# Two fused blocks on one core: GpSimd's elementwise work in 256-column pieces, and two waits of the schedule moved

## The chip, the cores and the metric

The kernel runs on one core of a Trainium2 chip, in one launch. The metric is device time in microseconds (us), the median of three executions. All durations below are from one profiled execution of the kernel before; times in it count from the start of its span.

## The reference

Two blocks follow each other on 256 tokens of width 1024. The first is a mixer (a gated causal convolution beside attention with a forget gate), cross attention to a memory, and a squared-ReLU MLP. The second is a state-space mixer with a short convolution, and then a product-key expert layer, which is the part that this study mostly speaks of:

```python
q = (t @ w_q).reshape(T, PEER_HEADS, 2, PEER_HALF)            # 8 heads
s = jnp.einsum('thsd,hskd->thsk', q, sub_keys)                # scores against 2 x 128 keys
v_half, i_half = lax.top_k(s, PEER_TOPK)                      # 16 of 128, per half
cand = v_half[:, :, 0, :, None] + v_half[:, :, 1, None, :]
best, pos = lax.top_k(cand, PEER_TOPK)                        # 16 of 256 pairs
experts = (i1 * PEER_KEYS + i2)                               # 16 experts per token and head
gates = jax.nn.softmax(best, axis=-1)
...
u = expert_u[eb]
act = jax.nn.gelu(jnp.einsum('td,tkd->tk', xb, u)) * gb
return jnp.einsum('tk,tkd->td', act, expert_v[eb])
```

Each of the 256 tokens reads 16 experts for each of 8 heads, and each expert is a row of u and a row of v, 1024 float32 numbers each.

## The kernel before

The 256 tokens are two tiles of 128 partitions. Nothing is issued where it is written: every operation is recorded in a `Plan`, and `Plan.schedule` places the recorded operations on the engines by a list scheduler with costs and priorities of its own, and `issue` then emits each engine's instructions in that order. Priorities come from the place of an operation in the program plus a shift for its block (`SHIFTS`, by block names such as `e03` or `scores1`). Some operations are recorded for `q.either` and may be placed on VectorE or GpSimd; `LATERS` holds for each block by how much the one engine must be ahead for the operation to go there. `q.wait` adds a predecessor that exists only for the scheduler: it moves instructions in the queues, and no engine waits for it at run time. All instructions are emitted from one line, so that the profile shows L519 nearly everywhere, and tiles tell them apart.

Matmuls in the first part take their weights in two parts: a rounded one, made by ScalarE, and the rest, made by a subtraction (`tensor_sub`) of 1024 columns on VectorE or GpSimd (`unit`). The scores of heads 1 to 7 use the same `unit` with `lead=0`; their subtractions go to VectorE alone, and they carry the scheduler's wait `q.place`.

The expert layer goes over tiles i and heads h in order; the blocks are e00 to e07 and e10 to e17 (tile, head). For each pair, `route` (blocks such as `route03`) finds the 16 experts of each token on VectorE from the scores `S[h]`; head 0 of tile 0 does it in haste, the first 8 experts ahead of the other 8. Then 16 gathers (`indirect_dma_start` on GpSimd's queue) each bring 128 rows of u and v, 2048 columns, into one of 10 row buffers. Per pair of rows VectorE makes the dot products (`dots`), ScalarE the gelu (`act`), VectorE multiplies by the gate, ScalarE scales the identity by the result (`dg`, two buffers), and TensorE multiplies `dg` with the v half and sums in two banks `acc`. The two matmuls that start `acc` add the residual `xt`. At the end of a tile the sum is normalised and stored. A row buffer is free for a later gather when the product has read it.

`HELD` weight units for the scores are loaded ahead and handed to `unit` through `early`.

Of the kernel before, what the change touches and what calls it, by code (L numbers as in the profile page):

```python
# [41 lines left out]
HELD = 10  # L42
# [37 lines left out]
    "attend21.te": 384, "mo.gp": 1722, "state3.ve": -1984, "ln.gp": 166, "dt.sy": 461, "dt.sc": 725,  # L80
# [127 lines left out]
class Plan:  # L208
# [163 lines left out]
    def schedule(self, window):  # L372
# [49 lines left out]
        while count < len(ops):  # L422
# [3 lines left out]
            for e in self.ENGINES:  # L426
                t0, pick = clock[e], None
                for i in cand[e]:
# [21 lines left out]
                    if not ok:  # L450
                        continue
# [1433 lines left out]
```

## Time and profile before

| | us |
|---|---|
| median of three runs | 1343.22 (1341.99 to 1345.15) |
| the profiled execution: its time | 1344.8 |
| its span in the profile | 1343.0 |
| first gather issued | 652.74 |
| last gather issued | 1314.08 |

The span is shorter than the time by what lies around it. The first 652.7 us hold the first block and the mixer of the second; the gathers of the expert layer take the rest.

### The profile page before, as it was taken

The numbers are of one execution on the slowest core, as the hardware profiler recorded it, in microseconds if no ns is written. First come the engines' busy times: TensorE is split into PE (matmuls) and PEld (weight loads), VectorE is DVE, ScalarE is ACT, GpSimd is POOL, SyncE is SP. The second block draws the span as 40 slices with busy tenths as digits, with TensorE's granted clock in tenths as the row PEclk, the third lists the DMA queues.
The fourth block names the chain that finished last, engine by engine and source line by source line (L and its number), as shares of the span: only waits on it lengthen the run. The fifth ranks groups of instructions, "written<-read, shape, count | busy, mean of one in ns | idle before, by whom it ended". The sixth has DMA issues, their size and how long they took to land.

```text
span 1343.0 us, 15842 instructions
## 1 busy us (share of the span) xinstructions
PE 1136.7 (85%) x5291; PEld 786.5 (59%) x5292; DVE 961.9 (72%) x2199; ACT 565.8 (42%) x1154; POOL 516.7 (38%) x405
## 2 busy tenths in 40 slices
PE   6998989999989989999497899887775977777776
PEld 5996778898969879988363555432332322222222
DVE  7988777555668887894789889997555455555555
ACT  6655565454545945653244444433222222112212
POOL 4731475220012574431333435554443533333330
PEclk9998999999989999999698999999997999999999
DMA  7432352555652334358588999999998999999996
GB/s 289 158 126 94 126 195 91 206 200 201 221 196 76 122 105 172 123 209 314 191 330 314 375 353 396 421 421 420 422 421 335 409 421 422 422 422 421 422 421 277
DMA packets 55701, 378.09 MB, mean 282 GB/s; under 512 B 6322, under 2 KB 6962, under 8 KB 11460
## 3 DMA queue, kind: packets, MB, share of 16 engines
q0 software_dynamic: 36864, 268.45, 48.8%
q1 hardware_dynamic: 18756, 108.63, 22.3%
q8 instruction: 42, 0.69, 0.2%
q14 instruction: 39, 0.32, 0.1%
HBM read 376.01 MB, written 1.05 MB: 281 GB/s over the span
## 4 chain that ended last, share of the span: by engine, by line
PE 37%; DMA 30%; DVE 17%; issue 7%; POOL 4%; ACT 4%; POOLq 0%; SPq 0%; DVEq 0%; ACTq 0%
DMA k<-in_uv,s_ei 28%; PE s L519 22%; PE mm L519 15%; DVE k L519 13%; POOL k L519 3%; ACT k L519 3%; DMA k<-in_wts 1%; DVE s_ix L519 1%; DVE s_v L519 1%; DMA x<-in_x 1%; DVE s_pos L519 1%; DVE act L519 1%; ACT L519 0%; DVE s_best L519 0%; POOL s_r L519 0%
## 5 line engine op out<-in xcount | busy, mean ns | idle before, releaser
L519 PE MATMUL s<-k,s_dg 128*128 128x512 f32 x1020 | 478.3, 616 | 148.6 <-ACT s_dg L519 148.4
L519 PEld LDWEIGHTS s<-k,s_dg 128*128 128x128 f32 x1020 | 189.8, 194 | 420.7 <-ACT s_dg L519 221.5
L519 DVE SCALAR_TENSOR_TENSOR k<-k,k 128x1024 bf16<-128x1024 f32 x256 | 312.9, 1222 | 168.5 <-DMA k<-in_uv,s_ei 167.9
L519 POOL DMA_INDIRECT k<-in_uv,s_ei x256 | 274.2, 1071 | 402.7 <-PE s L519 228.0
L519 PE MATMUL mm<-act,k 128*128 128x256 f32 (+4 forms) x2448 | 330.6, 288 | 2.7 <-ACT k L519 1.5
L519 PEld LDWEIGHTS mm<-act,k 128*128 128x128 f32 x2448 | 309.1, 189 | 17.1 <-issue 7.5
L519 ACT ACTIVATE k<-k 128x1024 fp32r<-128x1024 f32 (+9 forms) x293 | 230.3, 823 | 108.4 <-DVE k L519 63.8
L519 DVE TENSOR_TENSOR k<-k,k 128x1024 fp32r<-128x1024 f32 (+9 forms) x220 | 209.2, 982 | 45.7 <-ACT k L519 45.3
L519 POOL TENSOR_TENSOR k<-k,k 128x1024 fp32r<-128x1024 f32 (+4 forms) x84 | 180.5, 2166 | 152.8 <-ACT k L519 145.4
L519 PE MATMUL s<-k,k 128*128 128x512 f32 (+8 forms) x868 | 188.8, 362 | 10.7 <-DVE k L519 8.4
L519 ACT ACTIVATE s_act<-s_dots,rx 128x2 f32<-128x2 f32 x129 | 38.0, 294 | 337.1 <-DVE k L519 336.9
L519 PEld LDWEIGHTS s<-k,k 128*128 128x128 f32 (+2 forms) x868 | 145.2, 192 | 39.7 <-DVE k L519 9.5
L519 ACT ACTIVATE s_dg<-ident,s_act 128x128 f32<-128x128 f32 x255 | 91.6, 395 | 108.7 <-PE s L519 57.6
L519 PE MATMUL s<-k,act 128*128 128x512 f32 (+1 forms) x432 | 100.7, 382 | 1.6 <-ACT act L519 1.3
L519 PEld LDWEIGHTS s<-k,act 128*128 128x128 f32 x432 | 79.5, 193 | 13.0 <-ACT act L519 1.5
L519 ACT ACTIVATE k<-s 128x512 f32<-128x512 f32 (+10 forms) x99 | 46.3, 488 | 67.0 <-PE s L519 52.2
L519 DVE TENSOR_TENSOR k<-s,k 128x256 f32<-128x256 f32 (+8 forms) x100 | 45.1, 476 | 29.6 <-ACT k L519 21.2
L519 PE MATMUL s<-ident,k 128*128 128x128 f32 (+2 forms) x220 | 38.2, 302 | 26.9 <-DVE k L519 22.9
L519 ACT ACT_TABLE_LOAD x44 | 56.5, 1283 | 3.1 <-DVE s_mx L519 1.6
L519 ACT ACTIVATE k<-mm 128x256 f32<-128x256 f32 (+3 forms) x70 | 26.1, 373 | 67.8 <-PE mm L519 67.3
L519 POOL TENSOR_TENSOR s_r<-s_ms,nhalf 128x1 f32<-128x1 f32 x10 | 8.3, 835 | 102.2 <-DVE s_ms L519 98.5
L519 PEld LDWEIGHTS s<-ident,k 128*128 128x128 f32 (+2 forms) x220 | 27.5, 151 | 32.6 <-DVE k L519 25.0
(177 smaller groups left out, 778.9 us busy)
## 6 DMA issues: line engine op xcount, KB each, us to landing
k<-in_wts SPq DMA_DIRECT2D x89, 1024.0 KB, 4.8
k<-in_gains SPq DMA_DIRECT2D x9, 512.0 KB, 6.4
k<-in_uv,s_ei POOLq DMA_INDIRECT x256
k<-in_wts SPq DMA_DIRECT2D x12, 256.0 KB, 7.0
act<-in_wts SPq DMA_DIRECT2D x4, 512.0 KB, 9.4
x<-in_x SPq DMA_DIRECT2D x2, 512.0 KB, 6.7
k<-in_mem SPq DMA_DIRECT2D x2, 512.0 KB, 6.0
k<-in_sk SPq DMA_DIRECT2D x2, 512.0 KB, 6.0
```

Of the source, the lines that this page charges most:

```text
L519: getattr(getattr(self.nc, e), method)(*args, **kw)
```

## The change

There are four edits, and all numbers in `SHIFTS` (642 of 651) and most of `LATERS` (120 of 147) are other ones, so that all engines' queues are in a new order.

1. `cut`: an elementwise operation that is placed on GpSimd is emitted as pieces of at most 256 columns (`PIECE`). The scheduler's cost for GpSimd counts the pieces, and its rule for VectorE against GpSimd lets the other engine in between two pieces.
2. The wait of the matmuls that start `acc`: for the second tile it was the last recorded operation of the first tile, the store of its output; it is now `summed`, the last product of the first tile.
3. `q.place`, the wait of the scores of heads 1 to 7, was the last operation of the first two products of head 0, 1, 2 and 3; it is now the last operation of the scores of head 0.
4. `early.extend(held)` is done ahead of the loop.

```diff
+PIECE = 256
...
-            return 130 + 2.18 * n
+            return 130 * self.pieces(method, args, kw) + 2.18 * n
...
+    def pieces(self, method, args, kw):
+
+        if method not in ("tensor_sub", "tensor_mul", "tensor_add", "tensor_scalar") or "out" in kw:
+            return 1
+        shape = [c for _, c in args[0].ap]
+        if len(shape) == 2:
+            return max(1, -(-shape[1] // PIECE))
+        return max(1, -(-shape[1] * shape[2] // PIECE)) if len(shape) == 3 else 1
+
+    def cut(self, method, args, kw):
+
+        n = self.pieces(method, args, kw)
+        m = args[0].ap[1][1] if n > 1 else 1
+        step = -(-m // n)
+        for o in range(0, m, step):
+            yield args if n == 1 else tuple(
+                a[:, o:min(m, o + step)] if hasattr(a, "ap") and len(a.ap) > 1 and a.ap[1][1] == m else a
+                for a in args)
...
-                        r = max(r, lock["gpsimd" if e == "vector" else "vector"])
-                    s = max(r, t0)
+                        a, b, grain = lock["gpsimd" if e == "vector" else "vector"]
+                        if s < b:
+                            r = s = min(b, a + max(1, math.ceil((s - a) / grain)) * grain)
...
-                lock[e] = end
+                lock[e] = s, end, o.grain if e == "gpsimd" else 1e9
...
-            getattr(getattr(self.nc, e), method)(*args, **kw)
+            for a in self.cut(method, args, kw) if e == "gpsimd" else (args,):
+                getattr(getattr(self.nc, e), method)(*a, **kw)
...
     scores(0, whole=False)
+    early.extend(held)
+    st["next"] += HELD
+    q.place = q.last()
     q.block("experts")
...
-            q.wait = q.last()
+            q.wait = summed if i else q.last()
...
             if i == 0 and g == 0 and h < len(SCORES):
-                if h == 0:
-                    early.extend(held)
-                    st["next"] += HELD
-                q.place = q.last()
                 for x in SCORES[h]:
...
         if h == 7:
+            summed = q.last()
```

Of GpSimd's 66 elementwise operations on two tensors of 1024 columns, 44 stay and are emitted as four pieces each, and 22 go to VectorE; 12 multiplications of 256 columns go from VectorE to GpSimd.

The first place is the start of the second tile's head 0 (e10) on ScalarE. `s_act` is the gelu of two dot products, `s_dg` the scaled identity that a product waits for, and `k2` the square for the norm of the first tile. Before:

```order
L519 ACTIVATE s_act_2012<-s_dots_2007,rx1_1161 128x2
L519 ACTIVATE k2_2001,s_ss2_2000<-s_1220 128x512
L519 ACTIVATE k2_2002,s_ss2_2000<-s_1221 128x512
L519 ACTIVATE s_dg_2013<-ident_69,s_act_2012 128x128
L519 ACTIVATE s_dg_2014<-ident_69,s_act_2012 128x128
L519 ACTIVATE s_act_2020<-s_dots_2015,rx1_1161 128x2
L519 ACTIVATE s_act_2048<-s_dots_2043,rx1_1161 128x2
L519 ACTIVATE s_act_2056<-s_dots_2051,rx1_1161 128x2
L519 ACTIVATE s_act_2064<-s_dots_2059,rx1_1161 128x2
L519 ACTIVATE s_dg_2021<-ident_69,s_act_2020 128x128
```

Now:

```order
L548 ACTIVATE s_dg_2013<-ident_69,s_act_2012 128x128
L548 ACTIVATE s_dg_2014<-ident_69,s_act_2012 128x128
L548 ACTIVATE s_act_2020<-s_dots_2015,rx1_1161 128x2
L548 ACTIVATE s_dg_2021<-ident_69,s_act_2020 128x128
L548 ACTIVATE s_dg_2022<-ident_69,s_act_2020 128x128
L548 ACTIVATE s_act_2048<-s_dots_2043,rx1_1161 128x2
```

The scaled identity `s_dg_2021` stood behind three further gelus (of dot products of six later rows) and now follows its own.

The second place is TensorE between the scores of head 0 (`s_kp`) and the first product of the expert layer (the first row that names `s_dg`; `k_1223` is the first row buffer). `mm<-act` rows are matmuls for the scores of later heads. Before:

```order
L519 MATMUL s<-s_kp,k_1218 128x128 x2
L519 MATMUL s<-s_kp,k_1219 128x128
L519 MATMUL s<-x_63,ident 128x512 x2
L519 MATMUL s<-k_1223,s_dg 128x512 x2
L519 MATMUL s<-k_1224,s_dg 128x512 x2
L519 MATMUL s<-k_1259,s_dg 128x512 x2
L519 MATMUL s<-k_1260,s_dg 128x512 x2
L519 MATMUL s<-k_1287,s_dg 128x512
L519 MATMUL mm<-act,k_1236 128x256 x2
```

Now (the last rows ahead of the first product):

```order
L548 MATMUL s<-s_kp,k_1242 128x128
L548 MATMUL mm<-act,k_1475 128x256 x24
L548 MATMUL mm<-act,k_1250 128x256 x14
L548 MATMUL mm<-act,k_1479 128x256 x6
L548 MATMUL mm<-act,k_1250 128x256 x10
L548 MATMUL mm<-act,k_1479 128x256 x6
L548 MATMUL s<-s_kp,k_1252 128x128 x2
L548 MATMUL mm<-act,k_1479 128x256 x12
L548 MATMUL s<-s_kp,k_1253 128x128
L548 MATMUL s<-s_kp,k_1252 128x128 x2
L548 MATMUL s<-s_kp,k_1253 128x128
L548 MATMUL s<-k_1223,s_dg 128x512
```

Ahead of the first product stand 181 matmuls of the scores of heads 1, 2, 3 and 6, where none stood.

The third place is VectorE just ahead of the first list of experts, the cast to `s_ei_1199`, for which the first gather waits. Names with `s_v` and `s_ix` are another route's; rows that write a `k8` tile of 128x512 are the weights of the scores of heads 1 and 3, and `k1_1239` is a part of the scores of head 1. Before:

```order
L519 TENSOR_REDUCE s_pick_1196<-k2_1198 128x2x8
L519 CAST s_ixf_1935<-s_ix_1932 128x32
L519 TENSOR_TENSOR k1_1936<-s_v_1931 128x256
L519 SCALAR_TENSOR_TENSOR s_ef_1197<-s_pick_1196 128x8
L519 MAX_INDEX s_pos_1192<-s_best_1191,k1_1193 128x8
L519 MAX s_best_1937<-k1_1936 128x8
L519 CAST s_ei_1199<-s_ef_1197 128x8
```

Now:

```order
L548 TENSOR_REDUCE s_pick_1196<-k2_1198 128x2x8
L548 CAST s_abf_1195<-s_ab_1194 128x2x8
L548 TENSOR_SCALAR s_nb_1202<-s_best_1191,rx0_1160 128x1
L548 SCALAR_TENSOR_TENSOR s_ef_1197<-s_pick_1196 128x8
L548 TENSOR_TENSOR k2_1200<-s_abf_1195,iota16_76 128x128
L548 TENSOR_TENSOR k8_1348<-k2_1125,k8_1348 128x512
L548 TENSOR_TENSOR k1_1239<-mm_1237,k1_1238 128x256
L548 TENSOR_TENSOR k8_1348<-k2_1126,k8_1348 128x512
L548 CAST s_ei_1199<-s_ef_1197 128x8
```

Between the first maximum of this route and this cast stood 47 VectorE instructions, and now 52: eight more of the later heads' scores, eight fewer of the route of the second tile's head 0, and five more of this route's own second half.

Followed back through the queues and the waits, the first gather of e01, e02, e03, e04 and e05 has behind it 98, 168, 264, 349 and 447 VectorE instructions that come after those the first gather of all has behind it; now these are 91, 168, 200, 292 and 372.

## Rows read from the trace of the kernel before

**Rows 1.** The page: busy time by engine, and the gathers' DMA queue.
```profile
PE 1136.7 (85%) x5291; PEld 786.5 (59%) x5292; DVE 961.9 (72%) x2199; ACT 565.8 (42%) x1154; POOL 516.7 (38%) x405
...
q0 software_dynamic: 36864, 268.45, 48.8%
```
**Rows 2.** Windows (stretch, its length, busy us by engine, PE clock, DMA share, GB/s).
```profile
13.00:637.00 624.00, 592.60 (x3770) 532.65 (x3770) 472.32 (x842) 353.64 (x630) 233.98 (x130) 0.97 0.46 167
652.70:1343.00 690.30, 531.39 (x1448) 244.16 (x1448) 467.92 (x1273) 201.63 (x507) 276.30 (x258) 0.96 0.96 391
```
**Rows 3.** Windows from one head's first gather to the next's: e00 to e04, e10.
```profile
652.70:703.40 50.70, 36.13 (x156) 22.91 (x157) 38.72 (x125) 18.29 (x43) 20.34 (x18) 0.80 0.85 331
703.40:754.30 50.90, 41.12 (x145) 22.62 (x144) 46.32 (x157) 22.12 (x46) 18.01 (x17) 0.93 0.86 333
754.30:798.90 44.60, 39.38 (x160) 23.41 (x159) 37.63 (x120) 18.64 (x41) 18.75 (x16) 0.96 0.92 356
798.90:840.80 41.90, 39.69 (x158) 23.54 (x159) 40.53 (x135) 20.07 (x45) 19.72 (x16) 1.00 0.98 401
840.80:878.90 38.10, 33.00 (x96) 16.67 (x96) 38.10 (x148) 15.17 (x34) 19.94 (x16) 0.91 1.01 422
993.90:1045.20 51.30, 31.43 (x65) 12.84 (x66) 26.28 (x55) 12.77 (x35) 17.41 (x16) 0.87 0.88 357
```
**Rows 4.** Timeline of GpSimd: first gather, the one after the longest stop, last gather.
```profile
652.74 1.20 POOL L519 DMA_INDIRECT k<-in_uv,s_ei  x1 [17.02 <-DVE s_ab L519]
...
1038.37 0.93 POOL L519 DMA_INDIRECT k<-in_uv,s_ei  x1 [15.46 <-DVE k L519]
...
1314.08 0.94 POOL L519 DMA_INDIRECT k<-in_uv,s_ei  x1 [0.78 <-DVE k L519]
```
**Rows 5.** What TensorE's matmuls waited for, 13 to 637 us (us, times, longest).
```profile
PE s L519 <- DVE k L519: 31.5, 13, 12.6
```
**Rows 6.** Timeline of ScalarE at the start of e10.
```profile
1022.14 0.29 ACT L519 ACTIVATE s_act<-s_dots,rx 128x2 f32<-128x2 f32 x1 [4.11 <-DVE k L519]
1027.97 0.30 ACT L519 ACTIVATE s_act<-s_dots,rx 128x2 f32<-128x2 f32 x1 [5.54 <-DVE k L519]
1033.35 0.29 ACT L519 ACTIVATE s_act<-s_dots,rx 128x2 f32<-128x2 f32 x1 [5.08 <-DVE k L519]
1033.55 0.68 ACT L519 ACTIVATE s_dg<-ident,s_act 128x128 f32<-128x128 f32 x2
```
**Rows 7.** Timeline of TensorE: ends of three stops (idle before, and releaser).
```profile
503.42 2.34 PE L519 MATMUL s<-k,k 128*128 128x64 f32 x10 [5.75 <-DVE k L519]
...
666.85 3.78 PE L519 MATMUL s<-k,s_dg 128*128 128x512 f32 x4 [16.43 <-ACT s_dg L519]
...
1033.99 28.57 PE L519 MATMUL s<-k,s_dg 128*128 128x512 f32 x61 [13.19 <-ACT s_dg L519]
```
**Rows 8.** TensorE's groups by shape, 652 to 880 us (busy us, mean ns).
```profile
L519 PE MATMUL mm<-act,k 128*128 128x256 f32 x336 | 51.0, 301 | 0.5 <-ACT k L519 0.5
```
**Rows 9.** Timeline of VectorE: first maximum of the first route.
```profile
637.07 0.29 DVE L519 MAX8 s_v<-k 128x8 f32<-128x128 f32 x1 [0.85 <-ACT k L519]
```
**Rows 10.** Groups of elementwise instructions by shape (busy us, mean ns).
```profile
L519 POOL TENSOR_TENSOR k<-k,k 128x1024 fp32r<-128x1024 f32 x61 | 155.4, 2560 | 141.6 <-ACT k L519 137.1 <-issue 4.5
...
L519 DVE TENSOR_TENSOR k<-k,k 128x1024 fp32r<-128x1024 f32 x107 | 133.4, 1265 | 32.8 <-ACT k L519 32.7
...
L519 DVE TENSOR_TENSOR k<-k,k 128x256 fp32r<-128x256 f32 x34 | 21.5, 634 | 8.8 <-ACT k L519 8.6
...
L519 DVE TENSOR_TENSOR k<-k 128x256 f32<-128x256 f32 x28 | 19.7, 707 | 27.7 <-ACT k L519 27.7
...
L519 DVE TENSOR_TENSOR k<-mm,k 128x256 fp32r<-128x256 f32 x26 | 10.8, 418 | 3.9 <-ACT k L519 3.8
...
L519 DVE TENSOR_TENSOR k<-k,k 128x512 fp32r<-128x512 f32 x16 | 10.4, 685 | 1.8 <-ACT k L519 1.8
...
L519 POOL TENSOR_TENSOR k<-k,k 128x256 f32<-128x256 f32 x11 | 9.0, 828 | 1.2 <-PE s L519 1.0
```
**Rows 11.** Timeline of VectorE ahead of TensorE's stop at 497.7.
```profile
494.72 2.63 DVE L519 SCALAR_TENSOR_TENSOR k<-k,colt,k 128x256 f32<-128x256 f32 x1
...
500.28 3.09 DVE L519 TENSOR_TENSOR k<-k,k 128x768 fp32r<-128x768 f32 x1
```
**Rows 12.** Timeline of GpSimd at the same place.
```profile
493.94 3.12 POOL L519 TENSOR_TENSOR k<-k,k 128x1024 fp32r<-128x1024 f32 x1
```

More of the change, by code (lines that the diff above doesn't have):

```diff
@@ L1 @@
 import bisect
+import math
 from contextlib import ExitStack
@@ L52 @@
 SHIFTS = {
[27 rows of a table removed]
-    "attend21.te": 384, "mo.gp": 1722, "state3.ve": -1984, "ln.gp": 166, "dt.sy": 461, "dt.sc": 725,
[81 rows of a table removed]
-LATERS = {
[22 rows of a table removed]
[27 rows of a table added]
+    "attend21.te": 199, "mo.gp": 1828, "state3.ve": -2216, "ln.gp": -447, "dt.sy": -536, "dt.sc": 1092,
[83 rows of a table added]
+LATERS = {
[22 rows of a table added]
 SPAN = 3413.3
+PIECE = 256
 EARLY = {'s_kp': 3}
@@ L317, in add @@
             op.hold = 0.4167 * self.free(out) * args[2].ap[0][1] / P
+        op.grain = 1e9
+        if "gpsimd" in engs:
+            op.grain = self.cost("POOL", method, args, kw) / self.pieces(method, args, kw)
         op.table = None
@@ L393, in schedule @@
         table, dma = None, 0.0
-        lock = {"vector": 0.0, "gpsimd": 0.0}
+        lock = {"vector": (0.0, 0.0, 1e9), "gpsimd": (0.0, 0.0, 1e9)}
         cand = {e: [] for e in self.ENGINES}
@@ L451, in schedule @@
                         continue
+                    s = max(r, t0)
                     if o.lock:
-                        r = max(r, lock["gpsimd" if e == "vector" else "vector"])
-                    s = max(r, t0)
+                        a, b, grain = lock["gpsimd" if e == "vector" else "vector"]
+                        if s < b:
+                            r = s = min(b, a + max(1, math.ceil((s - a) / grain)) * grain)
                     p = o.prio
```

262 rows, old and new, of tables (LATERS, SHIFTS) are left out of this document.

## The prediction

> **What bounds the kernel now.** I read the page first: TensorE is busy for 85% of the span, no other engine for more than 72%, and one DMA queue, the gathers', carries 268.45 MB [rows 1]. These are averages over two unlike halves, so I cut the span at the first gather. From 13 to 637 us TensorE is busy for 592.6 of 624.0 us: this half is TensorE's, and only the 31.4 us in which it stands still are to be had. From 652.7 us to the end the DMA share is 0.96 and the mean rate 391 GB/s, with TensorE busy for 531 of 690 us: this half is the gathers' [rows 2].
>
> Next, the windows by head show where the gathers are not at their pace. In e04 they run at 422 GB/s with the DMA engines full. At that rate the 268.45 MB take 636.1 us, one of the 256 gathers 2.485 us and a head's sixteen 39.8 us. A window of length w at g GB/s loses w x (1 - g/422): e00 10.9 us, e01 10.7, e02 7.0, e03 2.1, together 30.7, and e10 7.9 [rows 3]. That is 38.6 of the 54.2 us by which the half (690.3) is longer than 636.1; the other 15.6 are its two ends: the first gather's way to its data, and what follows the last gather, issued at 1314.08. The longest idle time of the gathers' engine, 15.46 us, ends at 1038.37, in e10 [rows 4].
>
> Last, in the first half the waits of TensorE for VectorE add up to 31.5 us in 13 times; the longest, 12.6, is the start, which lies outside my window, and 18.9 are left [rows 5].
>
> **The second tile's start.** ScalarE makes a gelu at 1022.14, two more at 1027.97 and 1033.35, each after waiting 4 to 5.5 us for VectorE's dot products, and only then, at 1033.55, the scaled identities of the first [rows 6]. TensorE stands still for 13.19 us until 1033.99 and then does 61 products at one go [rows 7]: the row buffers came free late, and the gathers stopped. In the new order the identity follows its own gelu, so the product needs two dot products and no further six. The new wait itself costs nothing: the first tile's last product precedes the second tile's first on TensorE anyway. What is late next is VectorE's dot products, the same as in every head. I take the whole 7.9 us; the bounds are 0 (it returns elsewhere in e10) and 7.9, since a window cannot gain more than it lost. **-7.9.**
>
> **The start of the gathers.** TensorE ends a row of matmuls at 650.4 and then stands still for 16.43 us until the first product at 666.85 [rows 7]. Now 181 matmuls of later heads' scores stand there. At 51.0 us for 336 of this form they are 181 x 0.152 = 27.5 us [rows 8], so that they fill the stop and, if none ran earlier, end at 677.9. The first product frees the first of ten row buffers, which is wanted by the eleventh gather at 652.7 + 10 x 2.485 = 677.6. So this cover just suffices; without it each us of lateness would be a us of gathers. 27.5 us of scores are then gone from e00 to e03, where they stood in between.
>
> What sets how fast these heads can start is VectorE: the first gather of e05 came 226.2 us after the first of all (878.9 - 652.7), with VectorE busy for 201.3 of them by the five windows [rows 3], and 447 instructions stand behind it in the order, 0.506 us each. By that price the starts of e01 to e05 were due after 49.6, 85.0, 133.6, 176.6 and 226.2 us; they came after 50.7, 101.6, 146.2, 188.1 and 226.2, so e02 was 16.6 later than VectorE alone would make it. With the counts of now they are due after 46.0, 85.0, 101.2, 147.8 and 188.2; the pace of the gathers asks for 39.8, 79.5, 119.3, 159.0 and 198.8. VectorE is thus behind by 6.2 us at e01 and 5.5 at e02, and from e03 on ahead. The loss of the four windows, 30.7, falls to 6.2 at least, and to 22.1 if e02 starts as late as it did (101.6 against 79.5). I see no row that puts it nearer to one end, and take the middle, 14.1. **-16.6**, bounds 0 and -24.5.
>
> **The first list of experts.** The route's first maximum starts at 637.07 [rows 9]; the first gather is issued 15.7 us later, with 47 VectorE instructions in between. Now there are 52: eight more of the scores, of which I put four (512 columns) at 0.685 and four (256 columns, one operand in PSUM) at 0.418, together 4.4 us [rows 10], and three fewer small ones (eight fewer of another route, five more of its own second half), 3 x 15.7 / 47 = 1.0 us less. **+3.4**, bounds 0 and 6. The second half of the list is then nearer, so the second eight gathers do not wait for it.
>
> **Pieces on GpSimd.** An operation of 1024 columns takes it 2.56 us. The nearest row for a piece, 0.828 us for 256 columns, makes 3.31 for four; a quarter of the whole would be 0.64, and nothing extra. So 44 operations cost GpSimd 0 to 33 us more, 22 that leave give back 56, and 12 multiplications bring 10: it ends with less work. VectorE gets 22 x 1.265 = 27.8 us more and loses 12 x 0.42 to 0.71, so 19 to 23 more [rows 10]. In the first half VectorE is busy for 472 of 624 us and GpSimd for 234 [rows 2], so both fit beside TensorE; if the cover were gone, it is the third rival.
>
> What pieces can give shows ahead of TensorE's stop of 5.75 us, which ends at 503.42 [rows 7]. A VectorE operation of 256 columns took 2.63 us there, and one of 768 took 3.09 [rows 11], where 0.63 and (from 0.685 for 512) about 1.0 are usual [rows 10]. The first started while a GpSimd operation that ran from 493.94 for 3.12 us was under way, and ended just behind it [rows 12]. Pieces shorten what such an operation waits for from up to 2.56 to up to 0.83 us. I take the two excesses, 2.0 + 2.1, as gained. **-4**; bounds: -15.7, half of TensorE's idle time, and +27.8, all of VectorE's new work on the path.
>
> The Trainium skill, "SBUF — State Buffer", section "Who interferes with whom", says that a VectorE instruction with two SBUF inputs and a GpSimd instruction that reads SBUF shut each other out of a shared pair of ports, and that whichever issues first keeps it for the whole instruction. The overlap at 494.72 agrees with it. By that rule pieces shorten single waits but not the time for which GpSimd holds the pair, and VectorE, waiting between two pieces, in turn keeps GpSimd waiting; the sum for this term would be nearer to 0 than to -4.
>
> **The sum.** -7.9 - 16.6 + 3.4 - 4 = -25.1. The profiled execution took 1344.8, so 1319.7; it is 1.6 above the median of 1343.22, so I forecast **1318**. The own range of this case is 1306 (loss of 6.2 only, 4 more in the first half) to 1330.
>
> **Rivals.** *The gathers start as badly as before (0.17).* The 181 matmuls delay the first product past 677.6, or the second half of the list comes late, and row buffers run out in e00 to e02 as they did. For it: e02 was later than VectorE's work explains, so something else held it. Against it: the stop of 16.43 us is filled with work that was in the way later. Then only -7.9 - 4 + 3.4 = -8.5: 1335, from 1328 to 1343.
>
> *The first half gets shorter too (0.14).* With all queues in another order, half of TensorE's 31.4 us closes instead of 4: 11.7 more, 1306. For it: 18.9 us are waits for VectorE, which often waits for GpSimd. Against it: VectorE has some 20 us more to do.
>
> *VectorE's new work lands on TensorE's path (0.12), slower.* The subtractions moved to VectorE are weights that TensorE waits for; if they delay it where nothing else is ready, the first gather comes 27.8 us later: 1318 + 4 + 27.8 = 1350. It decides against the change from a first gather at 652.7 + 24.5 = 677.2 on, where the lateness eats the 7.9 and 16.6. For it: TensorE has only 5% to spare. Against it: VectorE has 24%.
>
> That the change does not do what it says has little room: the moved waits exist only in the scheduler, and the order shows the rows moved.
>
> **Chances.** The sum 0.57, rivals 0.17, 0.14 and 0.12. A measurement of this kernel can tell 0.2% (2.7 us) from no change. Faster by more: all of the first and the third case, most of the second, 0.83; within it 0.05, from the second; slower 0.12. The range reaches from 1301 to 1340: it leaves out the slow case and the edges of the others.
>
> **What would show it.** First gather near 652 (652.7 + 3.4 - 4); no stop of the gathers' engine over 8 us in e10, and e10's window near 43 to 44 us; windows e00 to e03 with 14 us lost in all, e02 and e03 above 400 GB/s; TensorE with no stop of 16 us ahead of its first product; VectorE's 256-column operations without 2.6 us cases; TensorE's idle time from 13 us to the first route near 27 in place of 31.4. A first gather behind 660, or e00 to e02 at 330 to 356 GB/s again, would make me wrong.

## The result

| | before | now |
|---|---|---|
| median, us | 1344.18 (1341.99 to 1348.15, 4 runs) | 1331.06 (1328.39 to 1332.22, 4 runs) |
| the profiled execution, us | 1344.8 | 1332.18 |
| its span, us | 1343.0 | 1330.4 |
| first maximum of the first route starts | 637.07 | 645.39 |
| first gather is issued | 652.74 | 663.95 |
| first gather to the end of the span | 690.3 | 666.45 |
| last gather issued to the end | 28.9 | 29.4 |

The ratio is 0.9896, 95% interval 0.9867 to 0.9926: 1.0% faster, some 13 us, and inside the range. The forecast of 1318 promised twice that. The two halves went opposite ways. The gathers' half got 23.8 us shorter (the forecast had 24.5), but it begins 11.2 us later (the forecast had 0.6 earlier). Timelines of VectorE and GpSimd now, the first maximum and the first gather:

```profile
645.39 0.29 DVE L548 MAX8 s_v<-k 128x8 f32<-128x128 f32 x1 [0.85 <-ACT k L548]
663.95 1.17 POOL L548 DMA_INDIRECT k<-in_uv,s_ei  x1 [20.29 <-DVE s_gr L548]
```

The page of the changed kernel, busy time by engine:

```profile
PE 1142.5 (86%) x5292; PEld 788.3 (59%) x5292; DVE 956.9 (72%) x2210; ACT 576.5 (43%) x1162; POOL 494.0 (37%) x542
```

Windows of the changed kernel: the first half up to the first maximum; then e00 to e03 and e10, each from the head's first gather to the next head's; then the stretch behind the last gather's issue (columns as in [rows 2]).

```profile
13.00:645.39 632.39, 599.80 (x3772) 536.05 (x3771) 469.53 (x854) 362.12 (x636) 211.33 (x267) 0.97 0.45 163
...
664.20:706.40 42.20, 38.73 (x197) 27.73 (x196) 37.80 (x118) 22.05 (x45) 17.48 (x17) 0.96 0.91 352
706.40:746.90 40.50, 39.52 (x155) 22.99 (x156) 39.23 (x139) 19.32 (x44) 18.93 (x17) 1.00 1.00 401
746.90:783.80 36.90, 35.43 (x142) 20.71 (x140) 35.48 (x117) 16.48 (x36) 21.45 (x17) 1.00 1.01 421
783.80:823.50 39.70, 32.13 (x89) 15.54 (x89) 39.30 (x145) 19.56 (x42) 19.00 (x17) 0.96 1.01 421
...
983.50:1025.80 42.30, 32.29 (x69) 12.97 (x68) 24.62 (x51) 12.27 (x33) 17.80 (x18) 0.96 1.01 422
...
1301.30:1330.40 29.10, 17.95 (x36) 7.18 (x36) 14.52 (x29) 6.21 (x18) 1.20 (x2) 0.86 0.43 176
```

By the prediction's own measure (length x (1 - GB/s / 422)) e00 to e03 lose 7.0, 2.0, 0.1 and 0.1 us, 9.2 in place of 30.7, and e10 nothing in place of 7.9 [rows 3]. That would be 29.4 us. But the last stretch, behind the last gather's issue, loses 29.1 x (1 - 176/422) = 17.0 us; before, at 255 GB/s in 28.9 us, it lost 11.4:

```profile
1314.10:1343.00 28.90, 16.52 (x36) 6.50 (x36) 14.45 (x29) 6.26 (x19) 1.49 (x2) 0.92 0.62 255
```

So 5.6 us are lost again there: -29.4 + 5.6 = -23.8, what the half got shorter.

In the first half TensorE works off the same matmuls (3770 recorded before, 3772 now), stands still for 32.6 us (31.4 before) and is busy for 599.8 us in place of 592.6 [rows 2]. Timeline of TensorE, its long stops in the first half and the start of the products:

```profile
74.58 10.49 PE L548 MATMUL mm<-act,k 128*128 128x256 f32 x82 [2.35 <-DVE k L548]
...
164.83 2.22 PE L548 MATMUL s<-ident,k 128*128 128x128 f32 x8 [6.26 <-DVE k L548]
...
508.44 1.30 PE L548 MATMUL s<-k,k 128*128 128x64 f32 x10 [2.12 <-DVE k L548]
...
676.57 6.32 PE L548 MATMUL mm<-act,k 128*128 128x256 f32 x36 [2.64 <-DVE k L548]
...
684.81 1.07 PE L548 MATMUL s<-k,s_dg 128*128 128x512 f32 x2
```

The stop of 16.43 us ahead of the first product [rows 7] is filled with scores. The stop that the prediction spoke of, at 503, is 2.12 in place of 5.75; a new one of 6.26 stands at 165.

### The profile page after: what moved, and what is told of

It reads as the page before. It is cut to its first block, busy times and chain, and to the rows that moved or that the text cites. A ratio compares the mean times of both kernels' runs of the same rounds, so it can differ in the third digit from the quotient of the medians.

```text
span 1330.4 us, 16001 instructions
## 1 busy us (share of the span) xinstructions
PE 1142.5 (86%) x5292; PEld 788.3 (59%) x5292; DVE 956.9 (72%) x2210; ACT 576.5 (43%) x1162; POOL 494.0 (37%) x542
## 4 chain that ended last, share of the span: by engine, by line
PE 39%; DMA 34%; DVE 15%; issue 5%; ACT 3%; POOL 3%; another core or an unknown queue 0%; SPq 0%; POOLq 0%; DVEq 0%; ACTq 0%
DMA k<-in_uv,s_ei 32%; PE s L548 22%; PE mm L548 17%; DVE k L548 11%; ACT k L548 3%; DMA k<-in_wts 2%; POOL k L548 2%; DVE s_ix L548 1%; DVE s_v L548 1%; POOL act L548 1%; DMA k<-in_ssdn 1%; DMA x<-in_x 1%; DVE s_pos L548 0%; ACT L548 0%; DVE act L548 0%
## 5 line engine op out<-in xcount | busy, mean ns | idle before, releaser
L548 PE MATMUL mm<-act,k 128*128 128x256 f32 (+4 forms) x2448 | 334.9, 289 | 9.0 <-DVE k L548 6.4
L548 PEld LDWEIGHTS mm<-act,k 128*128 128x128 f32 x2448 | 312.8, 191 | 25.0 <-DVE k L548 7.3
L548 ACT ACTIVATE k<-k 128x1024 fp32r<-128x1024 f32 (+11 forms) x293 | 231.3, 823 | 134.6 <-DVE k L548 58.1
L548 DVE TENSOR_TENSOR k<-k,k 128x1024 fp32r<-128x1024 f32 (+11 forms) x239 | 225.0, 970 | 51.7 <-ACT k L548 50.2
L548 POOL TENSOR_TENSOR k<-k,k 128x256 fp32r<-128x256 f32 (+2 forms) x205 | 160.7, 822 | 116.4 <-ACT k L548 100.2
L548 PE MATMUL s<-k,k 128*128 128x512 f32 (+8 forms) x868 | 191.5, 363 | 7.2 <-DVE k L548 3.6
L548 PE MATMUL s<-k,act 128*128 128x512 f32 (+1 forms) x432 | 103.6, 385 | 1.8 <-ACT act L548 1.3
L548 PE MATMUL s<-ident,k 128*128 128x128 f32 (+2 forms) x220 | 39.7, 308 | 30.0 <-DVE k L548 26.4
L548 POOL TENSOR_TENSOR s_rstd<-s_ms,nhalf 128x1 f32<-128x1 f32 (+1 forms) x15 | 16.1, 1071 | 115.9 <-DVE s_ms L548 115.6
```

The lines of the kernel that those rows point to most:

```text
L548: getattr(getattr(self.nc, e), method)(*a, **kw)
```

## The experiments

Each time is a median, with the ratio to the kernel before on the same chip. The kernels ran on several chips, on which the kernel before took 1343.3 to 1345.2 us. Where an experiment holds the order fixed, the operations are emitted from a written list, `ORDER`, of all 8110 operations in turn, instead of from the scheduler:

```diff
-        for _, _, i, e in self.schedule(window):
+        for t in ORDER.split():
+            i = int(t.rstrip("vg"))
+            e = {"v": "vector", "g": "gpsimd"}.get(t[-1], self.ops[i].engs[0][0])
```

**Pieces or order.** Two kernels keep every queue's order and change only whether GpSimd's operations are cut. `new_whole` is the changed kernel with

```diff
-            for a in self.cut(method, args, kw) if e == "gpsimd" else (args,):
-                getattr(getattr(self.nc, e), method)(*a, **kw)
+            getattr(getattr(self.nc, e), method)(*args, **kw)
```

and `old_cut` is the kernel before with the opposite edit and `pieces`, `cut` and `PIECE` of the change.

> The changed kernel with every queue in its order, but GpSimd's 44 operations of 1024 columns emitted whole again. In the changed kernel the first route's first maximum starts at 645.39 us, against 637.07 before, although TensorE has the same matmuls behind it. Theory A (the order of the first half, with 22 subtractions moved to VectorE, costs these 8.3 us; the pieces do little): first maximum at 643 to 648, time within 4 us of the changed kernel's 1331.1. Theory B (the pieces cost them: a piece takes 0.82 us, four 3.3 against 2.56 whole, and weights come later): first maximum at 637 to 640, time near 1324. Theory C (pieces help a poor order, as the prediction had it by 4 us): first maximum near 649, time near 1335.

> The kernel before with every queue in its order, but GpSimd's operations on two tensors emitted in pieces of 256 columns (66 of 1024 columns). Theory A (the order is at fault): time within 3 us of 1344.2, first maximum near 637. Theory B (the pieces are at fault): 8 us or more later, since it has 66 of them where the changed kernel has 44: first maximum at 645 to 650, time 1352 to 1357. Theory C (pieces help): the operation of 256 columns at 494.72 takes 0.7 to 1.4 us in place of 2.63, TensorE's stop of 5.75 us ahead of 503.42 gets 2 to 4 us shorter, time near 1340.

Measured: `new_whole` 1330.01 us (0.9899, 0.9882 to 0.9917), the same as the changed kernel; `old_cut` 1337.82 (0.9954, 0.9937 to 0.9970), some 6 us faster than before (5.5 by the medians, 6.2 by the ratio). Windows up to the first maximum, of `new_whole` and of `old_cut`:

```profile
13.00:645.07 632.07, 597.20 (x3773) 534.06 (x3774) 485.81 (x854) 362.19 (x636) 179.82 (x120) 0.97 0.45 163
```

```profile
13.00:629.80 616.80, 590.10 (x3773) 529.33 (x3773) 453.12 (x843) 353.39 (x630) 279.25 (x347) 0.98 0.47 169
```

In both orders the pieces save VectorE busy time, 485.8 to 469.5 and 472.3 to 453.1, and cost GpSimd some, 179.8 to 211.3 and 234.0 to 279.3. Ahead of the first maximum, 10 of VectorE's operations of 256 columns took over 2 us before, and 5 in `new_whole`; with pieces, in either order, none took over 1.03. TensorE's stops shrink too, from 31.4 to 26.7 us in the old order and from 34.9 to 32.6 in the new one. But the first maximum moves from 637.07 to 629.55 in the old order, and from 644.93 to 645.39 in the new one, where TensorE is busy for 2.6 us longer in the execution with pieces (its clock, below, differs between the two); the medians of `new_whole` and of the changed kernel show no gain either, to within some 3 us. Theory B is refuted by both kernels. Theory A, that the order is at fault, is right in the first; its forecast for `old_cut`, within 3 us of 1344.2, missed, and there theory C is right, by more than it said. The timelines of VectorE and TensorE in `old_cut` show where the old order gains:

```profile
494.69 0.47 DVE L540 SCALAR_TENSOR_TENSOR k<-k,colt,k 128x256 f32<-128x256 f32 x1
...
496.49 1.49 DVE L540 TENSOR_TENSOR k<-k,k 128x768 fp32r<-128x768 f32 x1
```

```profile
498.04 1.30 PE L540 MATMUL s<-k,k 128*128 128x64 f32 x10 [0.91 <-DVE k L540]
```

```profile
495.15 10.52 POOL L540 TENSOR_TENSOR k<-k,k 128x256 fp32r<-128x256 f32 x11
```

The same two VectorE operations took 2.63 and 3.09 us [rows 11]; TensorE's stop of 5.75 us has become 0.91. The last row is GpSimd's: its pieces run again from 495.15, so the operation at 496.49 ran beside them and the one at 494.69 did not.

**The halves joined.** `old_first` emits all operations that the first gather has behind it in both kernels in the order, and on the engines, of before, whole on GpSimd, and all others in the order of now. `old_first_cut` does the same with pieces:

```diff
-PIECE = 1 << 20
+PIECE = 256
```

> All operations that the first gather has behind it in both kernels in the order and on the engines of before, whole on GpSimd; all others in the order of now. If the two halves add up (first gather near 653 to 656 as before, then the 666 us of the changed kernel): 1343.2 + 3 - 24 = 1320 to 1324, faster than both kernels. If the gathers' half got faster only because the first half of now leaves it more work done ahead (57 operations more stand ahead of the first gather, 24 matmuls of scores among them): the windows of e00 to e02 lose more than the 7, 2 and 0 us of the changed kernel, and the time is 1328 to 1335.

> As old_first (operations ahead of the first gather in the order of before, the rest in that of now), with GpSimd's operations in pieces of 256 columns. In the order of before the pieces gave 6.2 us (1343.3 to 1337.8 by medians, first maximum from 637.1 to 629.8), so if this gain stands with the gathers' half of now: 1323.4 - 6.2 = 1317, from 1315 to 1319. If the gain is lost because the gathers start earlier than their rows come free: 1321 to 1324.

Measured: `old_first` 1323.43 us (0.9844, 0.9827 to 0.9860), as the sum of the two halves; `old_first_cut` 1317.04 us (0.9795, 0.9757 to 0.9833), faster than both kernels, 14 us below the changed one. The pieces are worth 6.4 us by the medians here. Windows of `old_first_cut`: first half, gathers' half, e00 and e01.

```profile
13.00:631.10 618.10, 589.99 (x3772) 529.15 (x3771) 452.87 (x843) 353.25 (x630) 279.57 (x347) 0.98 0.47 168
645.40:1315.40 670.00, 534.07 (x1446) 243.81 (x1446) 467.69 (x1288) 203.11 (x506) 278.76 (x258) 0.97 0.98 403
...
645.40:692.00 46.60, 45.41 (x250) 34.35 (x251) 43.26 (x138) 26.04 (x54) 20.64 (x17) 0.96 0.84 323
692.00:732.60 40.60, 38.70 (x155) 22.55 (x154) 38.40 (x134) 18.66 (x41) 18.72 (x16) 1.00 0.99 395
```

The gathers' half takes 670 us in place of 666, as 57 operations fewer stand ahead of the first gather. `old_n2_cut` puts these ahead again: old order up to the norm `n2`, new order from there.

> The order of before up to the second norm of the first tile ahead of the experts (block n2; 5326 of 8110 operations), that of now from there on, pieces of 256 columns. It differs from old_first_cut in the 57 operations (24 matmuls of the scores of head 1 and 19 operations on their weights among them) that stand ahead of the first gather again. If these are what old_first lacks in e00 and e01 (windows of 45.1 and 43.1 us against 42.1 and 40.5): first gather 3 us later, windows e00 and e01 5 us shorter, time 1314 to 1317 and 1 to 3 below old_first_cut. If they only shift work: the same time as old_first_cut within 1 us.

Measured: 1321.99 us (0.9833, 0.9795 to 0.9871), 5 slower than `old_first_cut`. The first maximum starts at 634.15 (631.03 there), the first gather 19.9 us later (14.4 there), and the windows e00 and e01 are 42.0 and 40.2 us long. The half from the first gather on is 4.3 us shorter, but it begins 8.7 us later. The extra work ahead of the first gather costs more than the windows give back; the expectation was wrong in its sign.

**Where the new first half loses.** `early_old` takes the old order up to the MLP (first matmul of `up1`) and the new one behind it, `late_old` the new order up to there and the old one from there to the first gather; `mid_old` is new up to the norm `ln` near 99 us, old up to `up1`, then new. All have pieces. `mv_back` is the changed kernel with 45 matmuls of the memory's values moved back.

> The order of before up to the first matmul of the MLP's first block (up1, at 219 us before and 227 now; 1836 operations), the order of now from there on, pieces of 256 columns. The first maximum stood at 631.1 with the whole first half in the old order and pieces, at 645.4 in the new one: 14.3 us to be placed. Theory A (TensorE loses its filler near 160 us, where 48 matmuls of the memory's values are done ahead of the wait that they filled before): 7 to 8 of the 14 go, first maximum at 637 to 639, time 1331.1 - 7.6 = 1323 to 1325. Theory B (the loss is made later, in the mixer): first maximum at 643 to 646, time 1329 to 1332.

> The complement of early_old: the order of now up to the MLP's first block (up1), that of before from there to the first gather, that of now behind it, pieces of 256 columns. If the two parts of the first half add up: early_old and late_old share the 14.3 us between them, with theory A 7 to 8 us here (first maximum at 638 to 640, time 1317.0 + 7.6 = 1324 to 1326). With theory B: first maximum at 631 to 633, time 1317 to 1319. If both early_old and late_old stay above 1328, the orders do not add up and each loses at the place where they are joined.

> The order of now up to the first matmul of the convolution's norm (ln, near 99 us; 883 operations), that of before from there to the MLP (up1), that of now from there on, pieces of 256 columns. Theory A (the filler of the wait near 160 us): the stop of 6.26 us that ends at 164.83 falls under 3, and the 5 us of lateness that arise between 99 and 219 us go; what arises ahead of 99 us (2.3 us) stays: first maximum at 639 to 642, time 1325 to 1328. Rival (what is late near 160 us is late because of the first 99 us): the stop stays above 5 us, time 1329 to 1332.

> The changed kernel with one move: the 45 matmuls that make the memory's values (block mv), which now all stand ahead of the transposes after the first norm (block seam1), stand again behind and between these transposes, as before. Theory A (TensorE has nothing to fill the wait of 6.26 us that ends at 164.83, since its filler was done too early; all of the 8.3 us of lateness at the first maximum is this): that wait falls under 2 us, first maximum at 638 to 640, time 1324 to 1326. Theory B (lateness has many causes in the new order, and a queue that gets ahead here waits later): first maximum at 643 or later, time 1328 to 1332.

| | median, us | ratio (95%) | first maximum |
|---|---|---|---|
| `old_first_cut` | 1317.04 | 0.9795 (0.9757 to 0.9833) | 631.03 |
| `late_old` | 1322.95 | 0.9837 (0.9816 to 0.9857) | 638.15 |
| `mid_old` | 1327.65 | 0.9870 (0.9848 to 0.9891) | 643.57 |
| `early_old` | 1328.30 | 0.9887 (0.9861 to 0.9914) | 640.31 |
| now | 1331.06 | 0.9896 (0.9867 to 0.9926) | 645.39 |
| `mv_back` | 1361.04 | 1.0133 (1.0092 to 1.0174) | 671.71 |

The loss is spread. Against `old_first_cut` the new order costs 5.9 us in the first third (`late_old`) and 11.3 behind it (`early_old`). Together that is 17.2, more than the 14.0 by which the changed kernel is slower, so that the parts do not quite add up, and neither theory had the split right. The filler at 165 us is not what makes the 8.3 us: `late_old` has the stop, `mid_old` does not, as their timelines of TensorE show, and the first maximum of `mid_old` comes only 1.8 us ahead of the changed kernel's. Two executions with the same order differ by more than that (3.5 us, see the last section). Its time of 1327.65 lies in the range of theory A, the first maximum does not.

```profile
166.01 2.22 PE L952 MATMUL s<-ident,k 128*128 128x128 f32 x8 [6.25 <-DVE k L952]
```

```profile
157.39 0.66 PE L952 MATMUL s<-ident,k 128*128 128x128 f32 x4 [0.70 <-DVE k L952]
157.81 4.42 PE L952 MATMUL s<-k,act 128*128 128x512 f32 x18
162.07 0.60 PE L952 MATMUL s<-ident,k 128*128 128x128 f32 x4
```

What TensorE does in the stop in one kernel it has done ahead of it in the other; the MLP begins at nearly the same time (225.7 in `late_old`, 225.9 in `mid_old`, 226.5 now). `mv_back` is a warning about moving one engine's work alone. Neither theory was near its 1361 us. From 140 to 170 us TensorE does 71 matmuls (95 in the changed kernel) and GpSimd nothing, with twelve matmuls at a time and a wait of about 1.2 us for ScalarE and 0.5 us or more for VectorE between them. A load of weights that is issued at 127.3 us in the changed kernel is issued at 148.0 here. Weights that were loaded early for the moved matmuls and hold the buffers which the next weights need would explain that; no run separates it.

**TensorE's clock in the first half.** TensorE is busy for 599.8 us in the changed kernel, 592.6 before and 590.0 in `old_first_cut`, for the same matmuls. About half of the difference to the kernel before, and most of that to `old_first_cut`, is pace. Its clock has two levels, 1.2 and 2.4 GHz, and the lower one (0.50 in the windows) was granted for 34.2 us of the first half before, 37.5 now and 27.3 in `old_first_cut`. The sums of the windows at that level, in this order:

```profile
sum 34.15, PE 25.65 PEld 21.96 DVE 27.98 ACT 14.28 POOL 5.45; mean PE 5.13 PEld 4.39 DVE 5.60 ACT 2.86 POOL 1.09
```

```profile
sum 37.54, PE 29.10 PEld 24.38 DVE 29.96 ACT 14.64 POOL 16.02; mean PE 4.16 PEld 3.48 DVE 4.28 ACT 2.09 POOL 2.29
```

```profile
sum 27.30, PE 18.15 PEld 14.57 DVE 20.71 ACT 10.46 POOL 7.92; mean PE 4.54 PEld 3.64 DVE 5.18 ACT 2.62 POOL 1.98
```

The start comes on top. Fifteen matmuls of 128x256 took 3.46 us in the changed kernel and 1.93 in `new_oldwait`, which has the same order there:

```profile
17.59 3.46 PE L548 MATMUL s<-act,thin 128*64 128x256 f32 x15 [0.52 <-DVE act L548]
```

```profile
17.49 1.93 PE L548 MATMUL s<-act,thin 128*64 128x256 f32 x15 [0.85 <-DVE act L548]
```

The windows read 1.00 there, but that is no reading: the trace has no record of the clock ahead of 21.9 us in the changed kernel (15.4 in `new_oldwait`, 17.7 before, 17.4 in `old_first_cut`). Up to that record the matmuls of 128x256 start 213 ns apart, as at the lower level; at the higher one it is 119. From 13 us to its first record TensorE was busy for 8.4 us now, 4.3 before and 4.1 in `old_first_cut`. An estimate from these rows: slow work of 37.5 us now (29.1 + 8.4), 30.0 before and 22.2 in `old_first_cut`, of which somewhat under half is lost, makes 3 to 4 us against the kernel before and about 7 against `old_first_cut`. The level goes with the order: 34.2 us of it in the kernel before and `old_summed`, 27.3 in the four others with the old first half (`old_cut`, `old_first`, `old_first_cut`, `old_n2_cut`), and 37.5 to 44.4 in the four with the new one (now, `new_whole`, `scores_back`, `new_oldwait`). The longest stretch at it now, from 161.9 us, begins within the stop that ends at 164.83. No run moves the clock by itself.

**The scores ahead of the first product.** `scores_back` moves one thing in the changed kernel: the 181 matmuls stand right behind the first product. Some VectorE and ScalarE instructions, most of which read their results, move with them (14 and 11 by the traces).

> The changed kernel with one move: the 181 matmuls of the scores of heads 1, 2, 3 and 6, which stand ahead of the first product, stand right behind it, and what reads them follows. Theory A (they gain because they fill TensorE's stop ahead of the first product): the stop of 13 to 16 us is back, the next products wait for 22 to 28 us of scores, e00 to e02 lose 10 us more of the gathers, time 1338 to 1345. Theory B (VectorE's share of work ahead of each head's first gather decides, and TensorE has time in e00 for either place): the windows of e00 to e03 stay within 2 us each, time 1329 to 1334.

Measured: 1347.95 us (1.0021, 1.0003 to 1.0039). Timeline of TensorE and the window of e00:

```profile
673.65 2.08 PE L952 MATMUL s<-k,s_dg 128*128 128x512 f32 x2 [18.99 <-ACT s_dg L952]
674.74 6.60 PE L952 MATMUL mm<-act,k 128*128 128x256 f32 x34
```

```profile
660.24:721.70 61.46, 46.35 (x251) 35.04 (x251) 40.11 (x120) 22.86 (x49) 16.72 (x17) 0.85 0.63 240
```

The stop is back with 18.99 us, and e00 loses 61.46 x (1 - 240/422) = 26.5 us in place of 7.0; the later windows are as they were. So the place of these matmuls, against this one other place, decides 19 us in e00 and 17 of the kernel's time. Theory A stands, and was too low; B falls.

**The second tile's wait.** `old_summed` is the kernel before with edit 2 alone; `new_oldwait` is the changed kernel without it:

```diff
-            q.wait = summed if i else q.last()
+            q.wait = q.last()
```

> The kernel before with only the second tile's wait changed (the sum waits for the first tile's last product); the orders of all engines are the same up to there. If the stop in e10 is the planner's doing alone and is not given back: e10's window 51.3 becomes 43 to 44 us, time 1344.2 - 7.9 = 1336. If something else holds the row buffers there (the norm of the first tile on VectorE and ScalarE): the stop stays at 8 us or more and the time between 1340 and 1344.

> The changed kernel with the second tile's wait of before; only ScalarE's order in e10 differs (23 rows of difference: three gelus ahead of the scaled identities again), TensorE's, VectorE's and GpSimd's orders are the same. If a stop in e10 costs what its window shows: e10's window from 42.3 to 50 us, time 1331.1 + 7.9 = 1339. If part of it is given back at the end (in the kernels without the stop the last transfers trail at 25 GB/s, a sixteenth of the full rate, for 5 us, and the stretch behind the last gather's issue lost 17.3 us against 11.4 with the stop): the stop is there, that loss falls back to 11 to 13, and the time is 1333 to 1336.

Measured: `old_summed` 1340.25 us (0.9971, 0.9960 to 0.9983), 3 to 4 us faster than before. The stop went, as in the first case of its expectation, but the time is that of the second case, in which the stop stays. `new_oldwait` took 1333.61 (0.9922, 0.9897 to 0.9948), 2.5 slower than the changed kernel and in the range of its second case; the intervals of the two kernels overlap, so that the 2.5 are not clear of noise. The windows of e10 and behind the last gather's issue, first of `old_summed`, then of `new_oldwait`:

```profile
993.30:1030.60 37.30, 29.46 (x66) 12.17 (x67) 21.18 (x45) 12.12 (x32) 17.57 (x17) 1.00 1.01 421
1308.00:1337.00 29.00, 16.59 (x36) 6.43 (x36) 14.45 (x29) 6.11 (x19) 1.34 (x2) 0.91 0.52 215
```

```profile
978.60:1032.90 54.30, 33.43 (x69) 14.08 (x68) 28.37 (x58) 13.15 (x35) 18.58 (x17) 0.81 0.85 345
1301.90:1330.50 28.60, 16.52 (x36) 6.51 (x36) 14.54 (x29) 6.26 (x19) 1.42 (x2) 0.92 0.62 258
```

With the stop, e10 loses 9.9 us in `new_oldwait` and the end 11.1; without it, in the changed kernel, 0.0 and 17.0. So 5.9 of the 9.9 us that the stop costs are saved again at the end. In the old order it is 7.9 and 11.4 with the stop, 0.1 and 14.2 without. How the end differs shows in the transfers' rates in 40 equal slices, GB/s, from 1290 us in `new_oldwait` (with the stop) and in the changed kernel (without):

```profile
GB/s 456 400 408 456 416 400 432 432 408 416 456 400 408 440 416 408 424 440 408 408 456 400 424 432 424 408 344 216 72 8 0 0 0 0 0 0 108 382 22 0
```

```profile
GB/s 440 416 408 440 408 424 432 416 424 416 432 400 416 440 408 424 440 408 424 384 328 160 88 48 24 32 24 24 32 0 0 0 0 0 0 0 194 318 0 0
```

A window of the changed kernel in the trailing stretch, and GpSimd's longest stop in `new_oldwait`:

```profile
1315.00:1319.00 4.00, 2.92 (x8) 1.12 (x7) 2.33 (x4) 0.99 (x3) 0.00 (x0) 1.00 0.06 27
```

```profile
1026.31 0.94 POOL L548 DMA_INDIRECT k<-in_uv,s_ei  x1 [19.03 <-DVE k L548]
```

With the stop all transfers end within some 4 slices of each other (a slice is 1.03 us). Without it the rate falls earlier, and then trails at 24 to 32 GB/s for five slices. That is about a sixteenth of 422 (26.4), and the DMA share is 0.06: one packet at a time, what one of the core's 16 DMA engines carries. The last row is complete only when that one is done, at the same 1320 us in both. By the packets, all eleven kernels without the stop in e10 end with 3 to 5 us of this, and none of the three with it (before, `old_cut`, `new_oldwait`) with more than 1.

## Why the prediction was right, and where it was wrong

**The halves.** The gathers' half came out at -23.8 against -24.5 by two misses that cancel: 4.9 us more were won in e00 to e03, and 5.6 were lost again at the end. That is luck. The start of that half is where the forecast failed: a first gather behind 660 was named as a sign of being wrong, and it came at 663.95.

**The start of the gathers (-16.6).** Right in its mechanism, and 21.5 by the windows. The first gathers of e01 to e05 came 42.2, 82.7, 119.6, 159.3 and 198.3 us after the first (706.4 to 862.5, less 664.2); due by VectorE's share were 46.0, 85.0, 101.2, 147.8 and 188.2, by the pace 39.8 to 198.8. So VectorE's share was over-priced by 4 us at the start, and from e03 on the pace rules, as worked out. The price of 0.506 us was elapsed time and not VectorE's; by its busy time, 201.3 / 447 = 0.450, e01 is due after 41.0 us, 1.2 behind the pace. The lower bound of 6.2 us for the loss (9.2 measured) was nearer than the middle that I took. The cover just sufficed, as worked out: the first product came at 684.8, 20.9 us after the first gather, inside the 24.9 us that the row buffers allow; and `scores_back` shows what the same scores cost behind it. What the new order of the lists on VectorE gives by itself no run separates.

**The second tile's start (-7.9).** The stop went as forecast, the time did not: "a window cannot gain more than it lost" is true, but the sum took the window's gain for the kernel's. In the changed kernel 5.9 of the 9.9 us won in e10 are lost again at the end, and the wait is worth 2.5 us by the medians, 3.7 (666.45 against 670.1) in the profiles; in the old order 3 to 4.

**The first list of experts (+3.4).** Right: 18.56 us in place of 15.67, +2.9.

**Pieces and the first half (-4).** This is the step that failed: the first half came out 8.3 us longer, a miss of 12.3, and with the 5.6 at the end and 4.9 the other way in e00 to e03 it makes the difference between the forecast and the result. The place and the mechanism were right: in the old order the pieces shorten the very operations and the stop named, and give some 6 us, more than the 4. But I priced a single stop of the old order and let everything else in the first half stand, while all queues there were in a new order. In that order the first maximum comes at 641.88 to 645.39 in four kernels that share it up to there (now, `new_whole`, `scores_back`, `new_oldwait`), with pieces or without, against 629.55 to 631.03 in the old order with pieces. No rival had that as its mechanism: the slower one put 27.8 us on VectorE's added subtractions, yet VectorE is busy for 469.5 us in the first half, less than before. TensorE's waits for VectorE, without the start, add up to 23.5 us, against 22.1 before. It is not one stop: the idle times are alike (32.6, 31.4, and 28.1 in `old_first_cut`), and TensorE is busy for 7 to 10 us more for the same matmuls. By the estimate above its pace makes 3 to 4 of the 7.2 us against the kernel before, and about 7 of the 9.8 against `old_first_cut`; the forecast had no term for the clock. Which of the scheduler's choices brought the slower stretches and the rest stays open.

**The rule on the shared ports.** An operation of VectorE still waits for a whole GpSimd instruction, but that is now a piece. The Trainium skill, "SBUF — State Buffer", section "Who interferes with whom", has the lock held for a whole instruction. The operation at 496.49, beside pieces, agrees with that (1.49 us, 3.09 beside whole operations); the one at 494.69 met no piece and tells nothing of it. The conclusion which I drew from the rule, that pieces would not shorten the sum of VectorE's waits, was wrong: VectorE's busy time fell by 16.3 and 19.2 us although GpSimd was busy for longer.

**Size against sign.** The sign held because the 23.8 us of the gathers' half are more than the 11.2 by which it begins later, and the halves are nearly independent: `old_first` gave the sum of the halves, 1323.4 where 1320 to 1324 were expected. The range held by its width; it was built from other cases than the one that came.

## What to carry to other kernels

When a change replaces the order of all queues, price the parts that it means to change, and keep apart a term for the parts that it merely reshuffles: here these ate half of the gain, and joining the old order of one half to the new order of the other gave 1317 us, the best of all kernels. A window that runs at full rate again is not yet time won; look at the end of the stream, where the slowest of the parallel transfers sets the finish. Work that fills a stop on one engine is worth what its lateness would cost elsewhere (17 us of the kernel's time here for 27.5 us of scores). When it is moved alone it can cost far more than the stop that it fills, as in `mv_back`. And look at the clock before a longer busy time is put down to the work.

## What the runs showed of the hardware

One of 16 DMA engines falls behind the others while the mean rate stays at 421 to 422 GB/s: the windows show nothing of it, only the end does, with 24 to 32 GB/s for 5 us. A stop of the gathers on the way (15.46 us before, 19.03 in `new_oldwait`) lets it catch up, so that part of such a stop is free. An early stop does not help: `scores_back` loses 26.5 us in e00 and trails at the end like the others. Which engine it is, and why it falls behind, no run shows.

A piece of 256 columns takes GpSimd 0.82 us (174 of them, mean 821 ns; 815 in `old_cut`), not the quarter of 2.56 us that is 0.64. That is near the upper of the bounds given, 0.828.

The first half of one order varies between profiled executions: with the same queues up to there the first maximum stood at 641.88 in `new_oldwait` and at 645.39 in the changed kernel. One source is the start, where TensorE ran at the slower pace up to 15.4 us in the one and 21.9 in the other, so that the 300th matmul came 2.0 us later; the granted clock of the windows does not show it, since the trace has no record of it that early.
